# Tiles of 520 columns, 512 of them used, for the weighted input and the gated products of the feed-forward layers

## The chip, the cores and the metric

The kernel runs on one core of a Trainium2 chip. The metric is the device time of one execution in microseconds. The time before is the median of three runs.

## The reference: what is computed

One sequence of 512 tokens with 1024 features goes through two blocks of layers, all in float32. The first block is a pair of macaron layers (feed-forward, mixer, feed-forward), with a state-space mixer (SSM) in the first and latent attention (MLA) in the second; so there are four feed-forward layers, called ffn00, ffn01, ffn10 and ffn11 here. The second block is a hybrid mixer and a mixture of 16 experts.

```python
def swiglu(h, w_gate, w_up, w_down):
    return (jax.nn.silu(h @ w_gate) * (h @ w_up)) @ w_down
...
for i in range(DEPTH):
    x = x + 0.5 * swiglu(rms_norm(x, norm_w[i, 0]), ffn_w_gate[i, 0], ffn_w_up[i, 0], ffn_w_down[i, 0])
    h = rms_norm(x, norm_w[i, 1])
...
    x = x + 0.5 * swiglu(rms_norm(x, norm_w[i, 2]), ffn_w_gate[i, 1], ffn_w_up[i, 1], ffn_w_down[i, 1])
```

The hidden width of a feed-forward layer is 2816, which is 22 blocks of 128.

## The kernel before

**Layout.** Features lie on the 128 partitions and the 512 tokens along them: `x` is eight tiles of 128 x 512. A matmul takes a weight block of 128 x 128 as the stationary operand and 512 columns of activations as the moving operand, and adds into one bank of PSUM.

**Three matmuls for a product.** Each float32 operand is split into a high and a low part of the type fp32r (`split`, L164 to L168: ScalarE's cast, CAST L166, and VectorE's difference, L167). `mm3` (L176 to L181) makes a product of three matmuls: L179 takes the high parts of both, L180 the high part of the weights and the low part of the activations, L181 the low part of the weights and the high part of the activations. In the profile these are `xh,wh`, `xl,wh` and `xh,wl`; the output is on the left of the arrow.

**Weights.** `Stream.load` (L97 and on) moves 1 MB pieces into the raw tiles by DMAs of the SP queue, and `Stream.next` splits a unit of 128 x 1024 into the tiles `wh` and `wl` of the pool `wp`.

**A feed-forward layer** (`ffn`, L272). `weighted_squares` (L232) multiplies the eight tiles of `x` by the gains of the norm, splits them into `xh0` to `xh7` and `xl0` to `xl7` (the pool `xw`, one slot for each), and sums the squares for the norm, whose factor is applied later. The 22 hidden blocks come in two halves, of 12 and of 10 blocks (L300). For each block `products` (L263) makes the gate and the up product, `ps_p`: 8 steps over the features with 3 matmuls each, 24 into one bank. `hidden` (L289) applies the norm's factor and the gate, and splits the gated product into `hh` and `hl` (the pool `fact`, 14 slots for each). At the end of a half `row_matmul` makes the down projection from the half's `hh`, `hl`: `row_steps` (L321) fills eight output blocks, `ps_d`, four banks at a time, and `evac` adds them to `x`.

**Who else uses these slots.** The sixteen slots of `xw` are shared. The SSM keeps its input and then eight of its sixteen gated output blocks (`ghi`, `glo`, `part`, L357) in them, the other eight in a pool of its own, `shp`. The MLA puts its compressed queries and keys (L712) and its attention output `oh`, `ol` (L876) there, and the hybrid mixer its modulated input (`modulated`, L1012). A slot is as wide as the widest tile that uses it. `ps_zdt` is a product of the SSM with the operands the other way round: 128 columns of `xh` are stationary and 288 columns of a weight tile move.

**The order.** PE's order is the one of the program text (`manual_schedule`); that of the other engines is made when the kernel is built, by a scheduler that knows where the tiles lie. The pools are stacked: those of a mixer or a layer lie behind `wp`, `xp`, `xw` and `nrm`, in that order, and the pool `tok`, which holds what the experts will need, grows from the other end of the memory (side="right"). `route_start` (L1554) makes the first things in `tok` while the layers before are still at work: it loads `gate_f` (L1564) and `wr`, the router's weights (L1566), by DMAs in ScalarE's queue, and computes `ps_rc` (L1569, eight matmuls) and `wg` (L1574) from `wr`. At the start of the hybrid mixer `modulated` turns `x` for the residual path (`ps_xt`, L1001), sums squares (`ssq`, L993), and gets the norm from `ps_ssq` (L206) and `ms` (L208); a chain of small VectorE steps for the recurrent unit (`lsp`, L600 to L608) runs at the same time. `alibi` (L1068) is a table that is loaded there.

```python
    def mm3(self, out, a, b, start, stop):
        (ah, al), (bh, bl) = a, b
        mm = self.nc.tensor.matmul
        mm(out, ah, bh, start=start, stop=False)
        mm(out, ah, bl, start=False, stop=False)
        mm(out, al, bh, start=False, stop=stop)
```

Of the kernel before, what the change touches and what calls it, by code (L numbers as in the profile page):

```python
# [9 lines left out]
F32R = mybir.dt.float32r  # L10
# [8 lines left out]
P = 128  # L19
S = 512  # L20
# [57 lines left out]
class Stream:  # L78
# [38 lines left out]
    def next(self, width, eng=None, pieces=1):  # L117
        raw = self.load(width)
        wh = self.pool.tile([P, max(width, 1024)], F32R, tag="wh", name="wh")
        wl = self.pool.tile([P, max(width, 1024)], F32R, tag="wl", name="wl")  # L120
        for i in range(pieces):
            c = blk(i, width // pieces)
            self.K.split(wh[:, c], wl[:, c], raw[:, c], eng)
        return wh, wl


class Kern:
# [104 lines left out]
    def weighted_squares(self, x, wcols, between=None):  # L232

        nc, pool = self.nc, self.nrm
        ssq = pool.tile([P, S], F32, tag="ssq", name="ssq")
        xw = []

        def square(d):
            if d == 0:
                nc.scalar.square(ssq, x[d])  # L240
            else:
                sq = pool.tile([P, S], F32, tag="sq", name="sq", bufs=2)
                if between and d > 3:
                    nc.gpsimd.tensor_mul(sq, x[d], x[d])
                else:
                    nc.scalar.square(sq, x[d])
                nc.vector.tensor_add(ssq, ssq, sq)

        for d in range(DB):
            hi = self.xw.tile([P, S], F32R, tag=f"xh{d}", name=f"xh{d}")  # L250
            lo = self.xw.tile([P, S], F32R, tag=f"xl{d}", name=f"xl{d}")
            i = self.scaled_split(hi, lo, x[d], wcols[:, d:d + 1])
            xw.append((hi, lo))
            if between is None:
                square(d)
            elif d in between:
                with self.tc.issue_after(i):
                    between[d]()
        for d in range(DB if between else 0):
            square(d)  # L260
        return xw, ssq
# [10 lines left out]
    def ffn(self, x, wcols, st, bg=None, between=None):  # L272

        nc = self.nc
        with ExitStack() as ctx:
            ctx.enter_context(self.tc.manual_schedule(engines={PE}))
            nrm = self.pool(ctx, "fnrm", 1)
            tmp = self.pool(ctx, "ftmp", 3)
            act = self.pool(ctx, "fact", 14)
            first = [st.next(1024, pieces=4) for _ in range(2)]  # L280
            xw, ssq = self.weighted_squares(x, wcols, between)
            r = None

            def evac(d, p):
                t = tmp.tile([P, S], F32, tag="t", name="t")
                nc.vector.scalar_tensor_tensor(t, p, 0.5, r, op0=ALU.mult, op1=ALU.mult)
                nc.vector.tensor_add(x[d], x[d], t)

            def hidden(pg, pu):  # L289
                g = tmp.tile([P, S], F32, tag="g", name="g")  # L290
                nc.vector.tensor_mul(g, pg, r)  # L291
                nc.scalar.activation(g, g, AF.Silu)
                h = tmp.tile([P, S], F32, tag="h", name="h")
                nc.vector.tensor_mul(h, pu, g)  # L294
                hh = act.tile([P, S], F32R, tag="ah", name="hh")
                hl = act.tile([P, S], F32R, tag="al", name="hl")
                self.split(hh, hl, h)
                hs.append((hh, hl))

            for f0, f1 in FF_HALVES:  # L300
                hs = []
                for f in range(f0, f1):
                    if f == 0:
                        p0 = self.products(2, first, xw, self.psum, *([[[k] for k in range(DB)]] if between else []))
                        rc = self.rstd_cols(ssq, D, self.pacc)
                        continue
                    pg = self.products(1, [st.next(1024)], xw, self.psum)
                    if f == 1:
                        r = self.to_rows(nrm, rc, ps=self.pacc)
                        hidden(*p0)  # L310
                    pu = self.products(1, [st.next(1024)], xw, self.psum)
                    hidden(pg[0], pu[0])
                    for _ in range(2 if bg else 0):
                        next(bg, None)
                self.row_matmul(hs, st, evac)
# [1837 lines left out]
```

## Time and profile before

| | |
|---|---|
| median of 3 runs | 2694.84 us (2693.6 to 2697.28) |
| profiled execution | 2697.9 us, of which span 2696.0 us |
| mean granted TensorE clock | 0.981 |
| PE busy | 2602.4 us, 97% of the span |
| DVE, ACT, POOL busy | 58%, 39%, 9% |
| mean DMA rate | 112 GB/s |

PE is TensorE's matmuls and PEld its weight loads, which run beside them; DVE is VectorE, ACT ScalarE, POOL GpSimd, SP the engine that only issues DMAs. A matmul's record lasts longer than the distance to the next one's start, since matmuls overlap in the array: the rhythm of a stretch of matmuls is the difference of two start times divided by the number of matmuls that start between them. A "q" behind an engine's name is its sequencer or DMA queue.

### The profile page before, as it was taken

The page shows a single profiled execution, that of the slowest core. Times are in us where ns is not written, and L with a number is a line of the kernel's source. Part 1 is how long each engine was busy: PE and PEld are TensorE (multiplying, and loading weights), DVE is VectorE, ACT ScalarE, POOL GpSimd, SP SyncE. Part 2 cuts the span into 40 slices and gives each one's busy share as a digit, 9 for nine tenths or more (in the row PEclk, how much of TensorE's full clock was granted, in tenths as well). Part 3 has the DMA queues.
Part 4 walks back from the last instruction along what each step waited for, and adds up shares of the span by engine and source line. Part 5 has one row for each costly group of instructions (what it writes and reads, how often), then busy time and mean ns, then how long its engine had stood idle before and what let it go on. Part 6 is the DMA issues. An engine that isn't in the chain of part 4 may idle for free.

```text
span 2696.0 us, 32260 instructions
## 1 busy us (share of the span) xinstructions
PE 2602.4 (97%) x12798; PEld 2144.4 (80%) x12798; DVE 1553.2 (58%) x2609; ACT 1059.9 (39%) x1789; POOL 230.5 (9%) x172
## 2 busy tenths in 40 slices
PE   8999999999999999999999999999999989997996
PEld 6888887888888888888888887888888878766774
DVE  5434357676766454657534367645434364767997
ACT  4322235645443222333322236643322234534674
POOL 0000001111110000000000003200000001303332
PEclk9999998999999999999999999999999989988998
DMA  4222321212134242534422222002222222115796
GB/s 153 94 94 97 106 83 62 79 63 79 63 134 149 102 160 96 183 130 146 167 94 94 94 85 78 17 23 104 94 94 98 106 84 92 48 40 188 254 338 197
DMA packets 57048, 300.77 MB, mean 112 GB/s; under 512 B 12066, under 2 KB 12578, under 8 KB 27706
## 3 DMA queue, kind: packets, MB, share of 16 engines
q1 hardware_dynamic: 49232, 281.21, 29.8%
q0 software_dynamic: 5328, 11.59, 1.5%
q10 hardware_dynamic: 2330, 5.84, 0.6%
q8 instruction: 102, 1.67, 0.2%
q14 instruction: 56, 0.46, 0.0%
HBM read 290.68 MB, written 15.75 MB: 114 GB/s over the span
## 4 chain that ended last, share of the span: by engine, by line
PE 86%; DVE 8%; DMA 3%; ACT 2%; issue 1%; SPq 0%; ACTq 0%; POOL 0%; DVEq 0%; POOLq 0%
PE ps_p L179 12%; PE ps_p L180 12%; PE ps_p L181 12%; PE ps_d L179 8%; PE ps_d L180 8%; PE ps_d L181 8%; PE ps_in L179 3%; PE ps_in L181 3%; PE ps_in L180 3%; DVE wl L167 3%; DMA expert_out<-ey,edst 2%; PE ps_s L833 1%; PE ps_o L859 1%; PE ps_y L541 1%; PE ps_z L180 1%
## 5 line engine op out<-in xcount | busy, mean ns | idle before, releaser
L166 ACT CAST wh<-raw 128x1024 fp32r<-128x1024 f32 (+3 forms) x494 | 485.6, 994 | 1130.7 <-PE ps_p L180 378.3
L167 DVE TENSOR_TENSOR wl<-raw,wh 128x1024 fp32r<-128x1024 f32 (+3 forms) x494 | 574.7, 1175 | 374.6 <-ACT wh L166 365.2
L179 PE MATMUL ps_p<-xh,wh 128*128 128x512 f32 x1408 | 550.2, 391 | 6.7 <-ACT xh L172 6.7
L180 PE MATMUL ps_p<-xl,wh 128*128 128x512 f32 x1408 | 550.0, 391 | 0.6 <-DVE xl L173 0.6
L181 PE MATMUL ps_p<-xh,wl 128*128 128x512 f32 x1408 | 549.4, 390 | 0.0
L179 PEld LDWEIGHTS ps_p<-xh,wh 128*128 128x128 f32 x1408 | 265.6, 189 | 62.7 <-ACT xh L172 6.7
L180 PEld LDWEIGHTS ps_p<-xl,wh 128*128 128x128 f32 x1408 | 265.3, 188 | 57.0 <-DVE xl L173 2.0
L181 PEld LDWEIGHTS ps_p<-xh,wl 128*128 128x128 f32 x1408 | 265.3, 188 | 55.3
L179 PE MATMUL ps_d<-hh,wh 128*128 128x512 f32 x704 | 279.1, 397 | 0.0
L181 PE MATMUL ps_d<-hh,wl 128*128 128x512 f32 x704 | 279.1, 396 | 0.0
L180 PE MATMUL ps_d<-hl,wh 128*128 128x512 f32 x704 | 279.1, 396 | 0.0
L294 DVE TENSOR_TENSOR h<-ps_p,g 128x512 f32<-128x512 f32 x88 | 60.8, 690 | 230.2 <-PE ps_p L181 229.8
L291 DVE TENSOR_TENSOR g<-ps_p,rb 128x512 f32<-128x512 f32 x88 | 60.3, 689 | 177.6 <-PE ps_p L181 177.6
L181 PEld LDWEIGHTS ps_d<-hh,wl 128*128 128x128 f32 x704 | 132.6, 188 | 32.3
L180 PEld LDWEIGHTS ps_d<-hl,wh 128*128 128x128 f32 x704 | 132.6, 188 | 32.3
L179 PEld LDWEIGHTS ps_d<-hh,wh 128*128 128x128 f32 x704 | 132.6, 188 | 32.2
L179 PE MATMUL ps_in<-xh,wh 128*128 128x512 f32 x336 | 140.9, 419 | 0.7 <-ACT wh L166 0.7
L181 PE MATMUL ps_in<-xh,wl 128*128 128x512 f32 x336 | 132.4, 394 | 0.5 <-DVE wl L167 0.5
L180 PE MATMUL ps_in<-xl,wh 128*128 128x512 f32 x336 | 132.1, 393 | 0.0
L181 PEld LDWEIGHTS ps_in<-xh,wl 128*128 128x128 f32 x336 | 63.6, 189 | 15.1 <-DVE wl L167 1.0
L962 DVE SCALAR_TENSOR_TENSOR macc<-mraw,c_act,macc 128x1024 f32<-128x1024 f32 x42 | 53.9, 1284 | 36.8 <-DMA mraw<-w_mod 36.2
L179 PEld LDWEIGHTS ps_in<-xh,wh 128*128 128x128 f32 x336 | 63.9, 190 | 12.9 <-ACT wh L166 1.1
(581 smaller groups left out, 4151.4 us busy)
## 6 DMA issues: line engine op xcount, KB each, us to landing
raw<-w_ffn SPq DMA_DIRECT2D x131, 1024.0 KB
raw<-w_moe SPq DMA_DIRECT2D x48, 1024.0 KB
raw<-w_ssm SPq DMA_DIRECT2D x31, 1024.0 KB
mraw<-w_mod SPq DMA_DIRECT2D x48, 512.0 KB
raw<-w_hyb SPq DMA_DIRECT2D x9, 1024.0 KB
expert_out<-zero SPq DMA_DIRECT2D x8, 512.0 KB
raw<-w_mla SPq DMA_DIRECT2D x4, 1024.0 KB
xtok<-expert_out POOLq DMA_DIRECT2D x8, 512.0 KB, 9.5
```

Source lines behind the costliest of these rows:

```text
L166: a = self.nc.scalar.copy(hi, src)
L167: b = (eng or self.nc.vector).tensor_sub(lo, src, hi.bitcast(F32))
L179: mm(out, ah, bh, start=start, stop=False)
L180: mm(out, ah, bl, start=False, stop=False)
L181: mm(out, al, bh, start=False, stop=stop)
L291: nc.vector.tensor_mul(g, pg, r)
L294: nc.vector.tensor_mul(h, pu, g)
L541: nc.tensor.matmul(py[:, blk(h, 64)], G[h][:, c], xdt[:, 4 * c + h], start=True, stop=True)
L833: nc.tensor.matmul(ps[:, :n], t["qT"][:, blk(i)], t["kT"][:, :n], start=True, stop=False)
L859: nc.tensor.matmul(t["po"][:, blk(i, 64)], t["pT", i][:, blk(j)], v[:, j, h], start=j == 0, stop=j == i)
L962: nc.vector.scalar_tensor_tensor(acc, w, ca[:, k:k + 1], acc, op0=ALU.mult, op1=ALU.add)
```

## The change

The tiles `xh0` to `xh7` and `xl0` to `xl7` that `weighted_squares` makes, and `hh`, `hl` in `hidden`, are allocated with 520 columns instead of 512, and the first 512 are used. A slot of these pools then takes 2080 bytes of each partition instead of 2048. The same instructions compute the same values.

```diff
         for d in range(DB):
-            hi = self.xw.tile([P, S], F32R, tag=f"xh{d}", name=f"xh{d}")
-            lo = self.xw.tile([P, S], F32R, tag=f"xl{d}", name=f"xl{d}")
+            hi, lo = (self.xw.tile([P, S + 8], F32R, tag=f"{t}{d}", name=f"{t}{d}")[:, :S] for t in ("xh", "xl"))
             i = self.scaled_split(hi, lo, x[d], wcols[:, d:d + 1])
             xw.append((hi, lo))
...
-                hh = act.tile([P, S], F32R, tag="ah", name="hh")
-                hl = act.tile([P, S], F32R, tag="al", name="hl")
+                hh, hl = (act.tile([P, S + 8], F32R, tag=t, name=n)[:, :S] for t, n in (("ah", "hh"), ("al", "hl")))
                 self.split(hh, hl, h)
```

**Where the tiles start.** The built programs place a tile at the same byte of every partition. Its start, as a remainder of 512, is:

| tile | before | with the change |
|---|---|---|
| `wh`, `wl` (pool `wp`) | 416 | 416 |
| `xh`d, `xl`d of `xw`, d = 0 to 7 | 416 each | 416 + 64d, 448 + 64d |
| `hh`, `hl` of `fact`, slot s = 0 to 13 | 64 each | 64 + 32s, 32s |
| `ghi`, `glo` in `shp` | 64 | 64 |
| weights `ow` of the hybrid mixer's out-projection, in tiles of their own (they move, against `yh`, `yl` in `xw`) | 32 | 32 |
| `eah`, `eal` of the experts (stationary; `wh` moves) | 352 | 352 |

The sixteen slots of `xw` grow by 512 bytes together, so everything behind them keeps its remainder. A block of 128 columns of a weight tile is 512 bytes wide and starts at the tile's own remainder. The slices of a weight tile that move in `ps_zdt` are 1152 bytes apart, so they start at 416, 32, 160 and 288 in turn, and each is used for 12 matmuls.

**What moves in the order.** With the change `fact` reaches to byte 204224 of a partition; `tok` begins at 203808 and has `gate_f` at 204448 in the kernel before. The scheduler puts `gate_f` and `wr` behind ffn11 for it. (Line numbers behind L251 are smaller by one, behind L296 by two, in the changed kernel.)

ScalarE, in the MLA mixer, before (`oh` is attention output, `ssq` the first square of ffn11):

```order
L849 COPY pTb<-ps_pT 128x512
L166 CAST wh<-raw 128x1024
L166 CAST oh_13901<-ps_oT 128x512
L1564 DMA gate_f<-modrow 128x1024
L1566 DMA wr<-w_router 128x160
L166 CAST wh<-raw 128x1024
L240 ACTIVATE ssq<-x_81 128x512
```

and with the change, at the end of ffn11 and the start of the hybrid mixer (`sq` are squares of the mixer's norm):

```order
L990 ACTIVATE sq<-x_87 128x512
L166 CAST wh<-raw 128x1024
L1562 DMA gate_f<-modrow 128x1024
L1564 DMA wr<-w_router 128x160
L1066 DMA raw<-alibi 128x2048
L990 ACTIVATE sq<-x_88 128x512
L1042 DMA gate_m<-modrow 128x1024
```

The two issues have moved behind the whole of ffn11, to the place right before `alibi`, whose own place is the same.

PE at the same point, before: half of `ps_rc` here, behind the last matmul of ffn11, the other half already amid its last down projection.

```order
L180 MATMUL ps_d<-hl,wh 128x512
L181 MATMUL ps_d<-hh,wl 128x512
L1569 MATMUL ps_rc<-wr,mod 128x20 x4
L1001 MATMUL ps_xt<-squares,x_81 128x128
L1001 MATMUL ps_xt<-squares,x_82 128x128
```

With the change:

```order
L180 MATMUL ps_d<-hl,wh 128x512
L181 MATMUL ps_d<-hh,wl 128x512
L1567 MATMUL ps_rc<-wr,mod 128x20 x8
L999 MATMUL ps_xt<-squares,x_81 128x128
L999 MATMUL ps_xt<-squares,x_82 128x128
```

All eight are now behind ffn11, with the sixteen `ps_xt` and then `ps_ssq` behind them. The rest of PE's order is the same.

VectorE, the norm's steps after the last `ssq`, before:

```order
L605 TENSOR_SCALAR lsp_o<-lsp_q 128x2
L607 SCALAR_TENSOR_TENSOR lsp_o<-lsp_o,lsp_q 128x2
L208 TENSOR_SCALAR ms<-ps_ssq 128x4
L607 SCALAR_TENSOR_TENSOR lsp_o<-lsp_o,lsp_q 128x2
L188 TENSOR_SCALAR rn_y<-ms 128x4
L607 SCALAR_TENSOR_TENSOR lsp_o<-lsp_o,lsp_q 128x2
L196 SCALAR_TENSOR_TENSOR rn_t<-rn_y 128x4
```

With the change:

```order
L1570 TENSOR_TENSOR rc<-ps_rc,rows 128x20
L599 TENSOR_SCALAR lsp_z<-lsp_e 128x2
L600 RECIPROCAL lsp_z<-lsp_z 128x2
L601 TENSOR_TENSOR lsp_z<-lsp_z,lsp_e 128x2
L602 TENSOR_TENSOR lsp_q<-lsp_z 128x2
L603 TENSOR_SCALAR lsp_o<-lsp_q 128x2
L605 SCALAR_TENSOR_TENSOR lsp_o<-lsp_o,lsp_q 128x2 x6
L605 SCALAR_TENSOR_TENSOR lsp_o<-lsp_o,lsp_z 128x2
L606 SCALAR_TENSOR_TENSOR lsp_o<-lru_nl,lsp_o 128x2
L1369 TENSOR_SCALAR lru_s_17000<-lsp_o 128x2
L208 TENSOR_SCALAR ms<-ps_ssq 128x4
L188 TENSOR_SCALAR rn_y<-ms 128x4
```

The whole `lsp` chain, and `rc`, which reads `ps_rc`, now stand before `ms`; before, `ms` and the steps behind it alternated with the chain's, and `rc` stood further up. On SP the issue of one weight load of the experts has moved behind the register load of `most_i`.

## Rows read from the trace of the kernel before

**Rows 1.** The page's head: the span, and each engine's busy time.
```profile
span 2696.0 us, 32260 instructions
...
PE 2602.4 (97%) x12798; PEld 2144.4 (80%) x12798; DVE 1553.2 (58%) x2609; ACT 1059.9 (39%) x1789; POOL 230.5 (9%) x172
```

**Rows 2.** The page's chain of waits that ended last, shares of the span by engine.
```profile
PE 86%; DVE 8%; DMA 3%; ACT 2%; issue 1%; SPq 0%; ACTq 0%; POOL 0%; DVEq 0%; POOLq 0%
```

**Rows 3.** Windows: stretch, length; PE, PEld, DVE, ACT, POOL busy; PEclk, DMA, GB/s.
```profile
60.00:140.00 80.00, 80.00 (x354) 66.24 (x353) 32.62 (x37) 23.87 (x30) 0.00 (x0) 1.00 0.29 104
```

**Rows 4.** The page's costliest groups: count, busy us, mean ns, idle before.
```profile
L179 PE MATMUL ps_p<-xh,wh 128*128 128x512 f32 x1408 | 550.2, 391 | 6.7 <-ACT xh L172 6.7
...
L179 PE MATMUL ps_d<-hh,wh 128*128 128x512 f32 x704 | 279.1, 397 | 0.0
...
L181 PE MATMUL ps_in<-xh,wl 128*128 128x512 f32 x336 | 132.4, 394 | 0.5 <-DVE wl L167 0.5
```

**Rows 5.** Timeline of PE, ffn00's second half: start us, length us, instruction.
```profile
216.35 0.40 PE L179 MATMUL ps_p<-xh,wh 128*128 128x512 f32 x1
...
217.05 0.39 PE L179 MATMUL ps_p<-xh,wh 128*128 128x512 f32 x1
...
325.17 0.40 PE L179 MATMUL ps_d<-hh,wh 128*128 128x512 f32 x1
...
381.40 0.29 PE L179 MATMUL ps_zdt<-wh,xh 128*128 128x288 f32 x1
```

**Rows 6.** Timeline of PE, SSM's out-projection: first of `shp`, first of `xw`, end.
```profile
788.52 0.40 PE L179 MATMUL ps_d<-ghi,wh 128*128 128x512 f32 x1
...
811.01 0.39 PE L179 MATMUL ps_d<-ghi,wh 128*128 128x512 f32 x1
...
832.78 0.40 PE L179 MATMUL ps_d<-ghi,wh 128*128 128x512 f32 x1
```

**Rows 7.** Timeline of PE, hybrid's out-projection (18 matmuls) and an expert's down projection.
```profile
2428.83 0.40 PE L179 MATMUL ps_out<-ow,yh 128*128 128x512 f32 x1
...
2432.79 0.40 PE L181 MATMUL ps_out<-ow,yl 128*128 128x512 f32 x1
...
2511.73 0.39 PE L179 MATMUL ps_d<-wh,eah 128*128 128x512 f32 x1
...
2513.79 0.39 PE L179 MATMUL ps_gu<-wh,eh 128*128 128x512 f32 x1
```

**Rows 8.** Timeline of PE, SSM's `ps_zdt`, slices at 160, 288, 416 and 32.
```profile
385.57 0.29 PE L179 MATMUL ps_zdt<-wh,xh 128*128 128x288 f32 x1
...
387.15 0.30 PE L179 MATMUL ps_zdt<-wh,xh 128*128 128x288 f32 x1
...
388.75 0.29 PE L179 MATMUL ps_zdt<-wh,xh 128*128 128x288 f32 x1
...
390.33 0.29 PE L179 MATMUL ps_zdt<-wh,xh 128*128 128x288 f32 x1
```

**Rows 9.** The tile `wr`, and timelines of ACT's queue, PE and DVE, hybrid's start.
```profile
L1566 ACTq DMA_DIRECT2D wr<-w_router x1: 449/449/449, 1801.5 to 1801.5; - x1
L1574 DVE TENSOR_TENSOR wg<-wr,mod x1: 325/325/325, 1805.2 to 1805.2; 128x160 f32<-128x160 f32 x1
...
2202.69 0.34 ACTq L1068 DMA_DIRECT2D raw<-alibi  x1
...
2201.74 0.96 PE L1569 MATMUL ps_rc<-wr,mod 128*128 128x20 f32 x8
2202.54 1.97 PE L1001 MATMUL ps_xt<-squares,x 128*128 128x128 f32 x16
2207.12 1.05 PE L206 MATMUL ps_ssq<-squares,ssq 128*128 128x1 f32 x8 [2.61 <-DVE ssq L993]
...
2210.46 0.16 DVE L208 TENSOR_SCALAR ms<-ps_ssq 128x4 f32<-128x4 f32 x1
```

**Rows 10.** The tile `most_i`: the register load in SP's queue.
```profile
L1760 SPq TENSOR_LOAD <-most_i x1: 484/484/484, 2493.3 to 2493.3; - x1
```

## The prediction

> **What bounds the kernel now.** I read the page's head first, then the chain of waits. TensorE is busy 2602.4 of 2696.0 us [rows 1], and 86% of the chain that ended last is PE's [rows 2]. What PE saves or loses while it runs without a gap is therefore saved or lost at the end. The windows view says whether it has gaps inside a feed-forward layer: in 60 to 140 us PE is busy for all 80.00 us, DVE for 32.62, ACT for 23.87, the DMA engines for 0.29 of the stretch, and the granted clock is 1.00, so the level is 2.4 GHz [rows 3]. Nothing there waits, and no other engine is near its limit. The rest goes by the rhythm of the matmuls, from one start to the next (the groups view gives 391 or 397 ns for a single one [rows 4], but they overlap, so what counts is the distance of starts).
>
> **The change, part by part.** No instruction is added or removed. Two things change: where tiles start within a partition, and the place of some instructions in the order.
>
> *1. The starts.* Every matmul reads a moving operand of 512 columns while the next weights are loaded, and the change shifts the moving tile against the weight tile. The trace already holds both relations. In a second half of a layer the up and gate products (10 blocks, 2 products, 24 matmuls: 480) run from 216.35 to 325.17, 226.7 ns each; the 240 matmuls of the down projection from 325.17 to 381.40 take 234.3 each [rows 5]. The moving tiles of the first start at 416 (mod 512), as the weights do; those of the second start at 64, 160 off mod 256. Form and weights are the same, so what differs is the tile that is read. The SSM's out-projection makes the trial cleaner: the same line, the same output, 96 matmuls from tiles of `shp` (64) from 788.52 to 811.01, 234.3 ns, and then 96 from tiles of `xw` (416) from 811.01 to 832.78, 226.8 ns [rows 6]. Two more distances: with the moving tile 128 from the stationary one, 17 steps of `ps_out` from 2428.83 to 2432.79 take 232.9 on average (233.5 taken); with 64 between them, 9 steps of `ps_d` take 228.9 each, from 2511.73 to the first `ps_gu` at 2513.79 [rows 7]. That it is the distance and not the region of memory is spoken for by `ps_zdt`: its moving operand runs through one weight tile in steps of 128 bytes mod 512, its stationary one stands still, and groups of 12 matmuls take 1.58, 1.60 and 1.58 us by turns: as the distance is 0, 128, 0 mod 256 [rows 8]. So I read a price per distance: 0 costs 226.7 ns, 64 costs 229, 128 costs 233.5, 160 costs 234.3; between them I interpolate 228 at 32 and 231.3 at 96.
>
> With the change the weights stay at 416, but the `xh` tiles stand at 64d and the `xl` tiles at 64d + 32 from them, and the `hh`, `hl` tiles run through all multiples of 32 too. All eight distances come up equally often. For 192 and 224 no row has a price. If it goes on rising (236, 238) the mean of the eight is 232.1; if it falls back to 0's (231.5, 229) it is 230.4. I take 231.2, the middle, since the last known step (128 to 160) is flat and decides for neither.
> - Up and gate products: 4 layers x 22 blocks x 2 x 24 = 4224 matmuls, 226.7 to 231.2, **+19.0 us** (bounds 230.4 and 232.1: +15.6 and +22.8).
> - Down projections: 4 x 22 x 24 = 2112, 234.3 to 231.2, **-6.5 us** (-8.2 to -4.6).
> - Other readers of the sixteen `xw` slots, which all become wider: `ps_in` has 1008 and a single one lasts 394 ns where `ps_p`'s lasts 391 [rows 4], so part of the price is paid already: at 228.4 now, +2.8. 192 of the SSM's out-projection and 192 of the MLA's at 226.7 now: +1.7. Small ones, where the tile is the stationary side: about +1. Together **+5.5 us** (0 to +7.5).
>
> What covers this: nothing. In these stretches PE has no idle time [rows 3], and the evictions, splits and weight loads on DVE, ACT and SP have more than half of their time free, so a PE that is 2% slower finds them ready as now.
>
> *2. The order at the start of the hybrid mixer.* The wider `fact` tiles reach into the space of `tok`, so `gate_f` and `wr` can be loaded only after ffn11 is done. In the trace `wr` is issued at 1801.5 and its reader starts at 1805.2, 3.7 us later; nobody else waits [rows 9]. Now the issue stands in ACT's queue right before that of `alibi` (2202.69 [rows 9]), so it lands near 2206.5. On PE the eight `ps_rc` (0.96 us) stand in front of the transposes; behind them `ps_ssq`, now at 2207.12 [rows 9], would start 0.96 + 1.97 us (the transposes) after 2206.5, at 2209.4: 2.3 late. On DVE the seven small `lsp` steps and two more, each about as long as `ms` (0.16 us [rows 9]) and 0.2 from start to start, now stand before `ms` (2210.46 [rows 9]), not between its successors: about 1.8 later, of which 0.6 comes back. These two delays lie beside each other, and the `xh` tiles, and so the hybrid's `ps_in`, wait for the later. **+2.0 us** (0, if the landing is as quick as PE's own way there, to 5). The SP and POOL queues: on SP one of the 1 MB weight loads of the experts moves behind the 0.48 us register load of `most_i` [rows 10]; the load is for work several units ahead, and one DVE split fewer lies before `most_i`, so I price it at 0 (-1 to +1). POOL's order is the same but for one memset that now waits, with no reader for long.
>
> *The sum:* 19.0 - 6.5 + 5.5 + 2.0 = **+20.0 us**. The profiled execution took 2697.9 us, 1.9 above its span [rows 1] and 3.06 above the median of 2694.84; so 2717.9 against its own time, and 2714.8 against the median. I say 2715.0.
>
> The Trainium skill, "SBUF — State Buffer", section "Who interferes with whom", gives TensorE two independent read ports, one for the moving operand and one for weight loads, and says that PE never waits on anyone. By it no distance could cost anything, and part 1 would be 0. Here [rows 6] is against it: 7.5 ns per matmul between two places of the same operand.
>
> **The rivals.**
> - *The region, not the distance.* The slow tiles `hh` and `shp` also lie far above the weights in a partition, the fast ones near by. If the region decides, nothing changes for either kind, since padding moves no tile to the other side; what is left is part 2: +2.0, 2696.8 against the median. For it: [rows 5, 6]; against it: [rows 8], where one and the same tile gives both rhythms, though by only 1.6 ns. The Trainium skill's rule above leads to the same time. Chance 0.15.
> - *The varied distances are cheaper than I think*, faster than before. Each distance now lasts for one or two matmuls, and if a conflict needs several to settle, the rhythm could stay near its lower end. The point from which it decides: 4224 (p - 226.7) + 2112 (p - 234.3) + 7.5 us spread over the rest is 0 at p = 228.1, or 229.2 without the last. At p = 227 it is +1.3 - 15.4 + 2.0 + 0.5 = -11.6, 2683. For it: the down projections have 7.6 ns to give. Against it: at the change from `ps_d` to `ps_p` the first three matmuls take 0.70 us, 233 each, before 226.7 is reached [rows 5], so a change of distance itself seems to cost, not to save. Chance 0.12.
> - *Every change of distance costs.* By that same row each matmul would be one of the first three after a change, near the top of the known prices: p = 234.3 throughout. +32.1 + 0 + 8.4 + 2.0 = +42.5, 2737. Chance 0.13.
>
> **How the numbers follow.** Forecast 0.60, the three rivals 0.15, 0.12 and 0.13. A measurement of this kernel tells 0.2%, 5.4 us, from no change. Faster by more than that takes most of the second rival, 0.10; the same, within 2689.4 to 2700.2, the first rival and the edge of the second and of the forecast, 0.20; slower 0.70. The forecast's own range is 2707 to 2723: the bounds of part 1 give -6 and +6 and part 2 has -2 and +3. The range for 8 in 10 leaves out the second rival and half of the third: 2693 to 2736.
>
> **What would show it.** Right: `ps_p` at about 394 to 396 ns a matmul where it is 391, `ps_d` of the feed-forward layers falling from 397 to about 394; 480 up and gate matmuls in 111 us, not 108.8; 240 of the down projection in 55.5, not 56.2; PE waiting 2 to 5 us at `ps_rc`, for the DMA of `wr`, behind the last `ps_d` of ffn11. If `ps_p` and `ps_d` both keep their rhythm, the region decides and I am wrong; if both come out near 227, the second rival holds; near 234, the third. A step that none of this covers would be PE idle inside a layer, with an eviction or a weight split as its releaser.

## The result and the profile after

The changed kernel takes 2711.83 us (median of 5 runs, 2705.82 to 2713.77); the kernel before, in the same number of runs, 2694.84 us. The ratio is 1.0065, with a 95% interval of 1.0053 to 1.0078: slower by 17 us (14 to 21), where 20 were forecast. The profiled execution took 2713.77 us.

The page's head, the chain's shares by engine, and the groups that answer to [rows 1, 2, 4]:

```profile
span 2711.9 us, 32260 instructions
...
PE 2619.6 (97%) x12798; PEld 2143.9 (79%) x12798; DVE 1553.9 (57%) x2609; ACT 1060.6 (39%) x1789; POOL 230.2 (8%) x172
...
PE 87%; DVE 6%; DMA 4%; ACT 2%; issue 1%; SPq 0%; ACTq 0%; POOL 0%; POOLq 0%; DVEq 0%
...
L179 PE MATMUL ps_p<-xh,wh 128*128 128x512 f32 x1408 | 555.1, 394 | 7.0 <-ACT xh L172 7.0
L180 PE MATMUL ps_p<-xl,wh 128*128 128x512 f32 x1408 | 557.2, 396 | 0.5 <-DVE xl L173 0.5
...
L179 PE MATMUL ps_d<-hh,wh 128*128 128x512 f32 x704 | 277.2, 394 | 0.0
...
L181 PE MATMUL ps_in<-xh,wl 128*128 128x512 f32 x336 | 132.9, 396 | 0.5 <-DVE wl L167 0.5
```

PE is busy 17.2 us longer with the same 12798 matmuls; DVE, ACT and POOL do what they did. The up and gate products have gone from 391 to 394 and 396 ns, the down projections from 397 to 394: up where the tiles used to agree with the weights, down where they did not. In the middle of the first layer the windows view has PE at 80.00 of 80.00 us as before, but with 347 matmuls where [rows 3] has 354:

```profile
60.00:140.00 80.00, 80.00 (x347) 65.04 (x347) 31.04 (x35) 22.54 (x29) 0.00 (x0) 1.00 0.29 101
```

So nothing waits, the granted clock is 1.00 as before, and each matmul is 2% further from the next. PE's timeline in ffn00, at the places of [rows 5] and at the first half's down projection:

```profile
150.89 0.39 PE L179 MATMUL ps_d<-hh,wh 128*128 128x512 f32 x1
...
217.67 0.40 PE L179 MATMUL ps_p<-xh,wh 128*128 128x512 f32 x1
...
328.73 0.40 PE L179 MATMUL ps_d<-hh,wh 128*128 128x512 f32 x1
...
384.36 0.29 PE L179 MATMUL ps_zdt<-wh,xh 128*128 128x288 f32 x1
```

480 up and gate matmuls now take 111.06 us, 231.4 ns each (226.7 before); the 288 and the 240 of the two down projections 231.9 and 231.8 each (234.3 before). A layer whose ends nothing disturbs, ffn10, takes 370.64 us from its first matmul to its last, not 367.05.

At the start of the hybrid mixer stands the wait that the moved load of `wr` makes; the tile view of `wr`, PE's timeline, and the windows view of the stretch of `ps_rc` (columns as in [rows 3]):

```profile
L1564 ACTq DMA_DIRECT2D wr<-w_router x1: 450/450/450, 2218.6 to 2218.6; - x1
L1572 DVE TENSOR_TENSOR wg<-wr,mod x1: 325/325/325, 2222.9 to 2222.9; 128x160 f32<-128x160 f32 x1
...
2218.03 0.40 PE L181 MATMUL ps_d<-hh,wl 128*128 128x512 f32 x1
2222.97 3.60 PE L1567 MATMUL ps_rc<-wr,mod 128*128 128x20 f32 x16 [4.54 <-DMA wr<-w_router]
...
2222.97:2226.57 3.60, 3.60 (x17) 3.60 (x18) 1.12 (x5) 1.69 (x3) 0.00 (x0) 0.50 0.82 340
```

PE sits idle for 4.54 us, and then `ps_rc` runs at the lower of its two clock levels, 1.2 GHz (granted clock 0.50): one matmul record lasts 381 ns by the tile view, where it was 266. The eight matmuls of `ps_rc` are sixteen records in the trace; the 0.96 us of [rows 9] are eight of them, and now all sixteen stand here. DVE's timeline, and then PE's at the hybrid's first `ps_q`:

```profile
2226.60 0.18 DVE L1570 TENSOR_TENSOR rc<-ps_rc,rows 128x20 f32<-128x20 f32 x1 [2.51 <-PE ps_rc L1567]
...
2230.78 0.16 DVE L208 TENSOR_SCALAR ms<-ps_ssq 128x4 f32<-128x4 f32 x1
...
2236.70 0.79 PE L1072 MATMUL ps_q<-xh,wh 128*128 128x512 f32 x1 [1.63 <-ACT xh L1012]
```

And PE's timeline before:

```profile
2201.51 0.39 PE L181 MATMUL ps_d<-hh,wl 128*128 128x512 f32 x1
...
2216.68 0.79 PE L1074 MATMUL ps_q<-xh,wh 128*128 128x512 f32 x1 [1.62 <-ACT xh L1014]
```

From the last matmul of ffn11 to the hybrid's first `ps_q` it is 18.7 us, not 15.2.

### The profile page after: what moved, and what is told of

It reads as the page before. It is cut to its first block, busy times and chain, and to the rows that moved or that the text cites. A ratio compares the mean times of both kernels' runs of the same rounds, so it can differ in the third digit from the quotient of the medians.

```text
span 2711.9 us, 32260 instructions
## 1 busy us (share of the span) xinstructions
PE 2619.6 (97%) x12798; PEld 2143.9 (79%) x12798; DVE 1553.9 (57%) x2609; ACT 1060.6 (39%) x1789; POOL 230.2 (8%) x172
## 4 chain that ended last, share of the span: by engine, by line
PE 87%; DVE 6%; DMA 4%; ACT 2%; issue 1%; SPq 0%; ACTq 0%; POOL 0%; POOLq 0%; DVEq 0%
PE ps_p L180 12%; PE ps_p L179 12%; PE ps_p L181 12%; PE ps_d L179 8%; PE ps_d L180 8%; PE ps_d L181 8%; DMA expert_out<-ey,edst 3%; PE ps_in L179 3%; PE ps_in L180 3%; PE ps_in L181 3%; DVE wl L167 2%; PE ps_s L831 1%; PE ps_o L857 1%; PE ps_y L539 1%; PE ps_z L179 1%
## 5 line engine op out<-in xcount | busy, mean ns | idle before, releaser
L179 PE MATMUL ps_p<-xh,wh 128*128 128x512 f32 x1408 | 555.1, 394 | 7.0 <-ACT xh L172 7.0
L180 PE MATMUL ps_p<-xl,wh 128*128 128x512 f32 x1408 | 557.2, 396 | 0.5 <-DVE xl L173 0.5
L181 PE MATMUL ps_p<-xh,wl 128*128 128x512 f32 x1408 | 554.5, 394 | 0.0
L179 PEld LDWEIGHTS ps_p<-xh,wh 128*128 128x128 f32 x1408 | 265.3, 188 | 70.2 <-ACT xh L172 7.0
L180 PEld LDWEIGHTS ps_p<-xl,wh 128*128 128x128 f32 x1408 | 265.3, 188 | 62.9 <-DVE xl L173 2.1
L181 PEld LDWEIGHTS ps_p<-xh,wl 128*128 128x128 f32 x1408 | 265.6, 189 | 60.2
L181 PE MATMUL ps_d<-hh,wl 128*128 128x512 f32 x704 | 277.4, 394 | 0.0
L180 PE MATMUL ps_d<-hl,wh 128*128 128x512 f32 x704 | 277.3, 394 | 0.0
L179 PE MATMUL ps_d<-hh,wh 128*128 128x512 f32 x704 | 277.2, 394 | 0.0
L180 PEld LDWEIGHTS ps_d<-hl,wh 128*128 128x128 f32 x704 | 132.2, 188 | 31.2
L179 PEld LDWEIGHTS ps_d<-hh,wh 128*128 128x128 f32 x704 | 132.2, 188 | 31.0
L181 PEld LDWEIGHTS ps_d<-hh,wl 128*128 128x128 f32 x704 | 132.2, 188 | 30.9
L179 PE MATMUL ps_in<-xh,wh 128*128 128x512 f32 x336 | 141.3, 421 | 0.7 <-ACT wh L166 0.7
L181 PE MATMUL ps_in<-xh,wl 128*128 128x512 f32 x336 | 132.9, 396 | 0.5 <-DVE wl L167 0.5
L180 PE MATMUL ps_in<-xl,wh 128*128 128x512 f32 x336 | 133.3, 397 | 0.0
L181 PEld LDWEIGHTS ps_in<-xh,wl 128*128 128x128 f32 x336 | 63.7, 190 | 15.5 <-DVE wl L167 1.0
L179 PEld LDWEIGHTS ps_in<-xh,wh 128*128 128x128 f32 x336 | 63.9, 190 | 13.9 <-ACT wh L166 1.1
```

## The experiments

The theory on trial: the rhythm is set by how far, mod 256 bytes, the moving tile starts from the weight tile, and the order at the hybrid's start adds a little. Against it: the region of memory; a cost of each change of distance; the start of the moving tile by itself; and, for the time, that the move of `wr` and not the rhythm makes it.

**One distance per layer (map_a, map_b).** Of the tiles that a matmul reads, only `hh` and `hl` move (`g`, `h` and `t`, which lie between `rb` and them, move along and are read by no matmul); `shift` is 96, 104, 112, 120 columns in map_a and 72, 80, 24, 88 in map_b, for ffn00, ffn01, ffn10 and ffn11. Every engine's order is that of before here and in all the maps.

```diff
-        rb = pool.tile([P, S], F32, tag=tag, name=tag)
+        rb = pool.tile([P, S + more], F32, tag=tag, name=tag)[:, :S]
...
-                        r = self.to_rows(nrm, rc, ps=self.pacc)
+                        r = self.to_rows(nrm, rc, ps=self.pacc, more=shift)
```

> The kernel before, with the tile rb of each feed-forward layer 96, 104, 112 and 120 columns wider (ffn00, ffn01, ffn10, ffn11), so that hh and hl of a layer all start 32, 64, 96 and 128 bytes (mod 256) from the weight tiles, not 160; nothing else moves. Distance theory (the distance of the moving from the stationary tile, mod 256, sets the rhythm): the down projections, now 234.3 ns from start to start, come to 228, 229, 231.3 and 233.5 ns in the four layers, about 56.2 us per second half turned into 54.7, 55.0, 55.5 and 56.0; whole kernel 2694.84 - 528 x (6.3 + 5.3 + 3.0 + 0.8) ns = 2686.7 us. Region theory (how far up in the partition the tile lies): 234.3 in all four, 2694.8 us. Theory that a change of distance is what costs: a constant distance costs little wherever it is, so all four lie near 227, except that it has no word for the 234.3 of before.

> The same edit with 112 - 64 + 24 = 72, 80, 24 and 88 columns: hh and hl start 192 and 224 bytes from the weights (mod 256) in ffn00 and ffn01, 256 bytes (mod 512; 0 mod 256) in ffn10, and 0 in ffn11. Distance theory: 226.7 ns in ffn11, the same 226.7 in ffn10 if the period is 256 (another value if it is 512), and for 192 and 224, of which no row tells, either 236 and 238 (goes on rising) or 231.5 and 229 (falls back). Region theory: 234.3 in all four layers.

PE's timeline of map_a, the first half's 288 down matmuls in ffn00 (distance 32) and ffn01 (64): the first of them, and the first matmul behind them.

```profile
149.14 0.40 PE L179 MATMUL ps_d<-hh,wh 128*128 128x512 f32 x1
...
216.34 0.40 PE L179 MATMUL ps_p<-xh,wh 128*128 128x512 f32 x1
...
987.74 0.40 PE L179 MATMUL ps_d<-hh,wh 128*128 128x512 f32 x1
...
1053.68 0.40 PE L179 MATMUL ps_p<-xh,wh 128*128 128x512 f32 x1
```

And of map_b, ffn10 (256 mod 512):

```profile
1354.36 0.39 PE L179 MATMUL ps_d<-hh,wh 128*128 128x512 f32 x1
...
1419.64 0.39 PE L179 MATMUL ps_p<-xh,wh 128*128 128x512 f32 x1
```

They give 67.20, 65.94 and 65.28 us, so 233.3, 228.9 and 226.7 ns. All distances, read in the same way (map_d is told below):

| distance | ns per matmul | where | the prediction took |
|---|---|---|---|
| 0, and 256 mod 512 | 226.7 | map_b, ffn11 and ffn10 | 226.7 |
| 8, 16 | 233.4, 231.7 | map_d, ffn00 and ffn01 | - |
| 32, 48 | 233.3, 233.3 | map_a, ffn00; map_d, ffn11 | 228 at 32 |
| 64 | 228.9 | map_a, ffn01 | 229 |
| 96 | 233.4 | map_a, ffn10 | 231.3 |
| 128 | 233.3 | map_a, ffn11 | 233.5 |
| 160 | 234.3 | kernel before | 234.3 |
| 192, 224, 240 | 233.3 each | map_b, ffn00 and ffn01; map_d, ffn10 | 231.5 to 236 and 229 to 238 |

The region theory falls: the same slots, moved by 96 or 352 bytes, go from 234.3 to 226.7. The period of 256 holds. But the price does not rise with the distance: 0 is cheap, 64 and 16 are less so, and everything else costs 233.3 to 234.3. The interpolated values at 32 and 96 were wrong. map_a took 2690.85 us and map_b 2683.2 us, one run each, beside one of the kernel before at 2687.09 us. Runs of that kernel differ by up to 12 us (2688.67 to 2700.48 in one set), so the maps are read by their rhythms and not by their times.

**Everything moved together (all_plus64).** One constant tile is 16 columns wider.

> One constant tile is 16 columns wider, so that every tile behind it, the weights, xh, xl, hh and hl alike, starts 64 bytes further up, and no distance changes. Distance theory: nothing changes, up and gate products 226.7 ns, down projections 234.3, 2694.8 us. If it were the start of the moving tile by itself (416 mod 512 fast, 64 slow): xh, xl at 480 and hh, hl at 128 would take other values, 227.5 to 236 for the first.

PE's timeline of all_plus64, ffn00's second half, at the places of [rows 5]:

```profile
215.24 0.40 PE L179 MATMUL ps_p<-xh,wh 128*128 128x512 f32 x1
...
324.05 0.40 PE L179 MATMUL ps_d<-hh,wh 128*128 128x512 f32 x1
...
380.28 0.29 PE L179 MATMUL ps_zdt<-wh,xh 128*128 128x288 f32 x1
```

The 480 up and gate matmuls took 226.7 ns each and the 240 down ones 234.3; the one run took 2696.43 us. The distance counts, not the start.

**Two distances in turn (map_c).** `hh` at 0, and a gap of 8, 32, 56 or 40 columns ahead of `hl`.

```diff
                 hh = act.tile([P, S], F32R, tag="ah", name="hh")
+                if wide[1] not in self.__dict__.setdefault("gaps", {}):
+                    self.gaps[wide[1]] = act.tile([P, (8, 32, 56, 40)[wide[1]]], F32, tag="gap", name="gap", bufs=1)
                 hl = act.tile([P, S], F32R, tag="al", name="hl")
```

> hh at distance 0 in all four layers (88 columns more in rb), and a gap tile of 8, 32, 56 and 40 columns between hh and hl, so that hl lies at distance 32, 128, 224 and 160 in ffn00, ffn01, ffn10 and ffn11. Of three matmuls in a row L179 and L181 read hh, L180 reads hl: the distance changes twice in three matmuls. If each matmul costs the price of its own distance, the down projections take (2 x 226.7 + price)/3: 227.1 at 32, 229.0 at 128, 229.2 at 160, and between 227.5 and 230.5 at 224. If a change of distance costs by itself, as the first three matmuls after a change in the kernel before say (233 ns): 231 to 234 in all four, and highest where the two distances differ most.

PE's timeline of map_c, the 288 down matmuls of ffn00 (0 and 32) and ffn01 (0 and 128), read as above:

```profile
147.14 0.39 PE L179 MATMUL ps_d<-hh,wh 128*128 128x512 f32 x1
...
213.86 0.39 PE L179 MATMUL ps_p<-xh,wh 128*128 128x512 f32 x1
...
985.45 0.39 PE L179 MATMUL ps_d<-hh,wh 128*128 128x512 f32 x1
...
1051.37 0.39 PE L179 MATMUL ps_p<-xh,wh 128*128 128x512 f32 x1
```

231.7 ns for 0 and 32, 228.9 for 0 and 128; 231.1 for 0 and 224, 232.2 for 0 and 160. The constant prices of the table, averaged two to one, would be 228.9, 228.9, 228.9 and 229.2. So neither side is wholly right. With 128 each matmul pays for its own distance (by line, averaged over the records' starts: L179 226.7, L180 234.3, L181 225.7), and the change is free. With the other three the mixture costs 2.2 to 3.0 ns per matmul more than its parts, and the lines with distance 0 are slowed too (231.8 and 230.1 at 0 and 32). The mixture comes near the constant price of its worse tile without reaching it. The one run of map_c took 2681.73 us.

**The weights' side (wl_128).** The tiles `wl` alone move by 128 bytes, with a gap that keeps the rest at 0.

```diff
+        if not hasattr(self.K, "gap"):
+            self.K.gap = self.pool.tile([P, 32], F32, tag="gap", name="gap", bufs=1)
         wl = self.pool.tile([P, max(width, 1024)], F32R, tag="wl", name="wl")
...
             x = [K.xp.tile([P, S], F32, tag=f"x{d}", name=f"x{d}") for d in range(DB)]
+            K.xp.tile([P, 32], F32, tag="gapx", name="gapx")
```

> A gap of 32 columns between the tiles wh and wl of the weight pool, and one that makes the shift of xw 256 bytes in all: wh, xh and xl lie at distance 0 of each other, wl 128 from all of them. Of three matmuls of ps_p, L179 and L180 use wh, L181 uses wl. If a matmul's price is set by the distance to its own weights, L181 is slow (from its start to the next start 233 ns, the others 227) and the mean is 228.9. If it is set by the distance to the weights that are loaded beside it, for the matmul behind it, L180 is the slow one, with the same mean. If both count, two of three are slow: 231. The down projections, with hh, hl at 160 from wh and 32 from wl: 233 to 234.3 either way.

PE's timeline of wl_128, ffn00's second half (its L181 is L179 of before), first `ps_p` and the first matmul behind the 480:

```profile
216.50 0.40 PE L181 MATMUL ps_p<-xh,wh 128*128 128x512 f32 x1
...
327.45 0.40 PE L181 MATMUL ps_d<-hh,wh 128*128 128x512 f32 x1
```

231.1 ns each, where 226.7 was. By line, over all starts in the trace: 227.0 for the first of three (own weights and next weights at 0), 232.5 for the second (own at 0, next at 128), 234.0 for the third (own at 128, next at 0). So neither the relation to the weights in use nor that to the weights loaded beside it decides alone: either would have left two of the three near 227. That both count fits the rows. That a change of the weights' own start from one load to the next costs would give the same two slow matmuls, and no run tells the two apart. One run took 2709.3 us, nearly as slow as the changed kernel, with every activation tile at its old distance from `wh`.

**In between (map_d).** `hh` and `hl` are slices of tiles of 576 columns, in 12 slots, and `shift` is 88 in all four layers, which alone would put them at 0.

```diff
-            act = self.pool(ctx, "fact", 14)
+            act = self.pool(ctx, "fact", 12)
...
+                o = (2, 4, 60, 12)[self.layer]
+                hh, hl = (act.tile([P, S + 64], F32R, tag=t, name=n)[:, o:o + S] for t, n in (("ah", "hh"), ("al", "hl")))
```

> Distances in between: hh and hl are slices of wider tiles (576 columns, 12 slots), which start 8, 16, 240 and 48 bytes from the weights (mod 256) in ffn00, ffn01, ffn10 and ffn11. In the first maps 0 gave 226.7 ns, 64 gave 228.9 and 32, 96, 128, 192 and 224 all 233.3. If 0 is one case and everything else the other: 233.3 in all four, or some value above 228.9. If the price grows with the distance from 0 and saturates by 32: near 228.4 at 8, 230 at 16 and at 240, 231 to 233.3 at 48. A value below 226.7 would give a faster kernel than distance 0 does.

8 gave 233.4, 16 gave 231.7, 240 and 48 gave 233.3. No smooth fall to 0, and nothing below 226.7. In act_to_0 (below) `rb` is as wide as here, so `g`, `h` and `t` stand the same; the 8 bytes of `hh` and `hl` alone make 233.4 of ffn00's 226.7. The one run took 2687.55 us (the kernel before 2691.86 beside it).

**The two halves of the change (xw_only, act_only).** Each takes one hunk of the diff alone; the order is that of before in both.

> Only the tiles of the weighted input are 520 columns wide; hh and hl keep their distance of 160, and every engine keeps the order of before. Distance theory: up and gate products 231.3 ns as in the changed kernel, down projections 234.3 as before; per layer +4.3 us, the SSM +2.8 and the MLA +1.1 as the changed kernel's trace has them, so +21 us: 2716. Theory that the 17 us of the change come from the order at the hybrid's start and from DMAs: near 2695.

> Only hh and hl are 520 columns wide, order as before. Distance theory: down projections 231.9 ns, not 234.3, 2112 x 2.4 = 5.1 us less: 2689.8, up and gate products 226.7 as before. Theory that padding these tiles does harm too: slower than before.

xw_only: 2713.93 us, ratio 1.0081 (1.0067 to 1.0094), which is +21.8 us (18 to 25). act_only: 2687.85 us, 0.9979 (0.9970 to 0.9988), -5.7 us (-8.1 to -3.2). Both as the rhythm says: ps_p 231.4 ns and ps_d 234.3 in the one, 226.7 and 231.8 in the other (ffn00's second half). Half of the change is a small gain; the other half costs nearly four times that.

**The starts without the move (after_13), and the move without the starts (order_only).** after_13 is the changed kernel with 13 slots for `hl`; order_only is the kernel before with `rb` of ffn11 256 columns wider.

```diff
-                hh, hl = (act.tile([P, S + 8], F32R, tag=t, name=n)[:, :S] for t, n in (("ah", "hh"), ("al", "hl")))
+                hh, hl = (act.tile([P, S + 8], F32R, tag=t, name=n, bufs=b)[:, :S] for t, n, b in (("ah", "hh", 14), ("al", "hl", 13)))
```

> The changed kernel with 13 slots for hl where 14 are given (a half has 12 blocks), so that the tiles end below the pool tok and every engine keeps the order of before: the starts alone, without the move of gate_f and wr. In the changed kernel's trace the hybrid's first ps_q is 3.5 us later against the end of ffn11 than before, and the hybrid's stage behind it 3.5 us shorter. If that is given back for good (work on other engines was waiting anyway), this kernel takes as long as the changed one, 2712. If the shorter stage is a chance of that execution, it is 3.5 us faster than the changed one: 2708.

> The kernel before with rb of ffn11 256 columns (1024 bytes) wider: all tiles keep their remainder of 512, but fact reaches into tok, so gate_f and wr are loaded behind ffn11 as in the changed kernel. Theory that the late load costs what it costs at its place: the hybrid's first ps_q 3.5 us later after the end of ffn11 (18.7 us, not 15.2), and the time 3.5 us longer, 2696.8 on a before of 2693.3. Theory that it is absorbed later: the same 18.7 us at the place, but no more time in all, 2693.3. Rhythms: 226.7 and 234.3 in both.

after_13: 2712.24 us, 1.0068 (1.0054 to 1.0082), +18.3 us. order_only: 2692.41 us, 0.9994 (0.9983 to 1.0005), -1.6 us (-4.6 to +1.3). So the starts make the whole of it as far as can be measured, and the move costs nothing that shows in the time, though at its place it costs more than was forecast. PE's timeline at the hybrid's start, first after_13:

```profile
2218.46 0.96 PE L1567 MATMUL ps_rc<-wr,mod 128*128 128x20 f32 x8
2219.27 1.96 PE L999 MATMUL ps_xt<-squares,x 128*128 128x128 f32 x16
2223.88 1.05 PE L206 MATMUL ps_ssq<-squares,ssq 128*128 128x1 f32 x8 [2.65 <-DVE ssq L991]
```

then order_only:

```profile
2203.53 3.49 PE L1572 MATMUL ps_rc<-wr,mod 128*128 128x20 f32 x16 [4.38 <-DMA wr<-w_router]
2206.84 3.65 PE L1004 MATMUL ps_xt<-squares,x 128*128 128x128 f32 x16
2210.29 0.95 PE L206 MATMUL ps_ssq<-squares,ssq 128*128 128x1 f32 x7
```

18.6 us from the last `ps_d` to `ps_q`, not 15.0 to 15.3 as in every kernel that keeps the order of before: 3.4 us lost. The time does not show them (-4.6 to +1.3). Where they may come back is read from single traces: at the start of the experts. DVE's and PE's timelines at the expert block that waits for `most_i`, after_13 with the order of before:

```profile
2506.37 1.22 DVE L167 TENSOR_TENSOR wl<-raw,wh 128x1024 fp32r<-128x1024 f32 x1 [0.78 <-ACT wh L166]
...
2507.77 0.15 DVE L1653 CAST most_i<-most 128x1 int32<-128x1 f32 x1
...
2508.51 0.77 PE L179 MATMUL ps_gu<-wh,eh 128*128 128x512 f32 x1 [2.52 <-DVE most_i L1653]
2509.07 0.63 PE L180 MATMUL ps_gu<-wl,eh 128*128 128x512 f32 x1
```

and order_only, where the moved weight load takes this split behind `most_i`:

```profile
2486.77 0.15 DVE L1658 CAST most_i<-most 128x1 int32<-128x1 f32 x1
2486.84 1.22 DVE L167 TENSOR_TENSOR wl<-raw,wh 128x1024 fp32r<-128x1024 f32 x1
...
2487.51 0.47 PE L179 MATMUL ps_gu<-wh,eh 128*128 128x512 f32 x1 [0.99 <-DVE most_i L1658]
2487.82 0.40 PE L180 MATMUL ps_gu<-wl,eh 128*128 128x512 f32 x1
```

The split of 1.22 us no longer stands ahead of `most_i`. PE waits 0.99 us, not 2.52, and its next matmuls last 0.40 us at a granted clock of 1.00 (2.4 GHz; windows view, 2.5 us from 2487.50), where after the longer wait they last 0.63 at 0.50 (1.2 GHz; 2.5 us from 2508.50). The third group of `ps_gu` then starts 14.6 us after the first in order_only and 15.1 in the changed kernel, where it is 17.2 to 17.9 in the ten other kernels of this section: 2 to 3 us, about what was lost before. The kernel before has 15.5 in its own profile, after a wait of 1.9 us; act_only has 17.2 after the same wait, and what differs is that the matmuls behind it last 0.40 us in the one and 0.63 in the other. So a part of this differs from one execution to another, and against the trace of the kernel before the gain is only 0.4 to 0.9 us. That the split's place is a cause is read from these rows; it was not tried by itself.

**A version that beats both (act_to_0).** The same `more` as in the maps, 88 columns in all four layers, and 88 unused columns ahead of the SSM's `shp`; every down projection and the whole SSM out-projection come to distance 0.

```diff
+            self.pool(ctx, "spad").tile([P, 88], F32, name="spad")
             hp = self.pool(ctx, "shp", 8)
```

> No tile is padded, but the space ahead of hh, hl (88 columns more in rb) and ahead of the SSM's tiles in shp (an unused tile of 88 columns) puts them at distance 0 from the weights, as xh and xl are. Distance theory: all down projections at 226.7 ns, 2112 x 7.6 = 16.0 us, and 192 matmuls of the SSM's out-projection, 1.5 us: 2694.8 - 17.5 = 2677.3. Theory that other waits take the place of what PE saves: less than half of that.

2674.91 us, ratio 0.9930 (0.9916 to 0.9943): 18.9 us faster than before, and 37 us faster than the changed kernel by the medians. PE's timeline, ffn00's first down projection:

```profile
148.74 0.39 PE L179 MATMUL ps_d<-hh,wh 128*128 128x512 f32 x1
...
214.02 0.39 PE L179 MATMUL ps_p<-xh,wh 128*128 128x512 f32 x1
```

65.28 us for 288: 226.7 ns.

## Why the prediction was right, and where it was not

- **What bounds it: right.** PE without a gap, 2.4 GHz, and every ns of the rhythm on the path. PE's busy time has grown by 17.2 us, the time by 17.
- **Up and gate products, +19.0 us: right.** Their start-to-start in the changed trace is 231.3 ns on average, 231.2 were taken.
- **Down projections, -6.5 us: right in sign, 1.4 us too large.** 231.9 ns, so 2112 x 2.4 = 5.1 us; act_only has 5.7 (3.2 to 8.1).
- **The other readers of the slots, +5.5 us: too large.** From the first `ps_zdt` to ffn01 it is 2.8 us more than before, from the end of ffn10 to ffn11 1.1 more: 3.9, and nothing that could be told apart in the hybrid. The three terms come to +17.8; after_13, which has them without the move, is 18.3 us slower.
- **The order at the hybrid's start, +2.0 us: failed as a term of the sum.** The delay at its place is there and larger, 3.4 us. The step that priced PE's way took 0.96 us for all of `ps_rc`, where [rows 9] show half of its sixteen records, and took them at 2.4 GHz: all sixteen took 3.60 us, at a granted clock of 0.50. And DVE's delay does not stand by itself beside PE's, as the prediction has it: in DVE's order `rc`, which reads `ps_rc`, stands ahead of the `lsp` chain and of `ms`, so the chain starts only when `ps_rc` is done (2226.60). `ms` comes 12.75 us behind the last `ps_d`, where it came 8.95 behind it. In the time none of this shows: order_only has -1.6 (-4.6 to +1.3). The step that priced SP's moved weight load at 0 (-1 to +1) may be what failed there: in the traces it goes with a DVE split out of the way of `most_i` and 2 to 3 us less at the experts' start than in ten of eleven kernels without it. That this pays for the delay is not shown.
- **The prices behind 231.2: right by luck.** Those taken at 32 and 96 were too low (228 and 231.3; 233.3 and 233.4 measured). With the measured ones the mean of the eight distances is 232.1, the upper bound of the forecast. But the eight do not come up equally often in the up and gate products: `xh`, at 0, 64, 128 and 192, is read by two matmuls of three, `xl`, at 32, 96, 160 and 224, by one. With these weights the measured prices give 231.6, and 231.3 was measured. So the low prices took 0.9 ns from the mean, counting the distances equally put 0.5 on it, and the mixture itself stays 0.3 below the mean of its parts. Why it does is left open: map_c shows mixtures above the mean for three pairs, and at it for one.
- **The rivals.** The region falls with map_b. Cheaper mixtures fall with 231.3, above the 228.1 from which the forecast would have turned. That each change costs is half right: in map_c a change between 0 and 32, 160 or 224 does, one between 0 and 128 does not; but the 234.3 throughout that this rival took did not come.

The Trainium skill, "SBUF — State Buffer", section "Who interferes with whom", has the ports for the moving operand and for weight loads independent, and PE waiting on nobody. The runs speak against it as a rule for timing: 352 bytes more room ahead of a tile changed 234.3 to 226.7 ns per matmul (act_to_0), and moving only the weights of one matmul in three changed 226.7 to 231.1 (wl_128). Which reads get in each other's way, no run shows.

## What to carry to other kernels

Where PE runs without a gap, read its rhythm from start to start, by the tiles that it reads: two rhythms for the same form of matmul at the same granted clock are a reason to look at the placement. For fp32r matmuls with a weight load each and 512 moving columns, the form tried here: lay the moving tiles at the same remainder of 256 bytes as the weight tiles (here an unused strip ahead of a pool is enough), and keep the pitch of slots a multiple of 256; a pad that makes each slot start elsewhere put both kinds of product at 231 to 232 ns. And when a change moves a slot's end, look at what a neighbouring pool's tiles then have to wait for, and follow the order on every engine to the end, as a loss of 3.4 us at one place did not show in the time here.

## What the runs showed of the hardware that was not expected

- The price of a distance is nearly two-valued: 226.7 ns at 0 (mod 256), 228.9 at 64, 231.7 at 16, and 233.3 to 234.3 at all nine others tried, 8 among them.
- With the low weights 128 bytes off (wl_128), two of three matmuls slow down (232.5 and 234.0 ns, 227.0 the third), the one that uses them and the one during which they are loaded.
- The same work behind ffn11 differs from one execution to the next by more than the 3.4 us that the moved load of `wr` costs at its place. The windows view of the hybrid's stretch from the first `ps_q` to the first `ps_out`, the kernel before and then act_only, which does the same there, one execution each:

```profile
2216.68:2427.47 210.79, 204.39 (x997) 157.95 (x997) 136.48 (x312) 93.86 (x230) 40.43 (x22) 0.93 0.17 59
```

```profile
2210.59:2415.73 205.14, 198.71 (x996) 153.95 (x997) 136.03 (x312) 93.86 (x230) 40.43 (x22) 0.96 0.18 61
```

5.65 us apart, at a granted clock of 0.93 and 0.96. A comparison of two single traces up to the end of ffn11 (2201.51 and 2218.03, 16.5 us) says more of this change than the one of their spans.
